# A rotary-embedding kernel on one Trainium2 core: half of tile 0 by SyncE's queue, GpSimd's loads after a wait, frequencies first

**Chip, cores, metric.** One core of one Trainium2 chip. The metric is the device time of the launch in microseconds, median of several runs. The profile covers a slightly shorter span of the same execution (83.5 us where the run took 85.3). The experiments ran on three chips (a, c and d on one, b on the second, e on the third), each beside its own runs of the kernel before (medians 85.43 to 85.64), so the ratios compare across them better than the times.

## The reference

```python
# x: (8, 8, 1024, 64) f32; freqs: (32,); positions: (1024,)
angles = np.outer(positions, freqs)
cos, sin = np.cos(angles), np.sin(angles)
x_first, x_second = x[..., :32], x[..., 32:]
out = concat([x_first * cos - x_second * sin, x_first * sin + x_second * cos], axis=-1)
```

It reads 16.8 MB and writes 16.8 MB.

## The kernel before

x is cut into 8 tiles of 2 MB (128 partitions of 64 rows x 64 values). GpSimd's DMA queue loads them and casts f32 to bf16, VectorE rotates in bf16, and GpSimd's queue stores them, casting back. SyncE's queue, which copies f32 without a cast, brings the first 16 of 64 rows of tile 0 and takes away the last 24 rows of tile 7. The parts that matter here:

```python
piece = 8
head = 2 * piece
x0 = singles.tile([P, head, d], f32)
for r in range(0, head, piece):                      # SyncE: 2 loads of 256 KB
    nc.sync.dma_start(out=x0[:, r:r + piece], in_=hbm(x, 0, r, r + piece))
# ... ScalarE's queue: positions (4 small loads), then freqs (1 small load)
for g in range(ntiles):                              # GpSimd: everything else of x
    lo = 0 if g else head
    nc.gpsimd.dma_start(out=xts[g][:, lo:], in_=hbm(x, g, lo))
# ... VectorE: positions * freqs, range reduction; ScalarE: sin_h, cos_h
nc.scalar.copy(out=xts[0][:, :head], in_=x0)         # f32 -> bf16
# ...
tail = 3 * piece
for g in [1, 0] + list(range(2, ntiles)):            # VectorE rotates, GpSimd stores
    hi = C if g < ntiles - 1 else C - tail
    ot = opool.tile([P, C, d], bf16, name="ot")[:, :hi]
    rotate(g, 0, hi, ot)
    ots.append(ot)
    nc.gpsimd.dma_start(out=hbm(out, g, 0, hi), in_=ot)
# ... the last `tail` rows as f32; SyncE waits for all stores but the last tile's, then:
#     sp.dma_start(...) for each piece of `last`
```

## Time and profile before

| | before |
|---|---|
| time, median of three runs (range); 85.64 with the fourth | 85.62 us (85.57 to 85.75) |
| span of the profile | 83.5 us |
| VectorE busy | 63.5 us |
| DMA: GpSimd's queue / SyncE's queue | 24.12 MB / 1.31 MB |
| VectorE ends / SyncE issues its last stores / last packet ends | 74.5 / 77.76 / 82.1 us |

In the profile's DMA rows a casting load is counted by the bf16 bytes that it writes, so 215 GB/s in the load half means 430 GB/s of reading. The timeline of GpSimd's queue (start, length, engine, line, operation, operands, count, and in brackets the idle time before and what ended it) shows when the loads are queued:

```profile
1.25 4.38 POOL L74 DMA_DIRECT2D xt<-in_x_dram  x8 [0.80 <-PEq L170]
```

All eight are queued one after another from 1.25 us on, so from then the queue stays deep. The waits of VectorE (line, what it waited for, total, times, longest) show the price of that: the tiny positions loads come late among the big packets.

```profile
DVE pos_i L76 <- DMA pos_i<-in_positions_dram: 8.0, 1, 8.0
```

### The profile page before, as it was taken

To read this page: it belongs to the slowest core of one execution; us is meant where nothing else is said; L and a number is where in the kernel's file an instruction comes from. 1 tells how busy PE (TensorE), PEld (TensorE's weight loads), DVE (VectorE), ACT (ScalarE), POOL (GpSimd) and SP (SyncE) were. 2 spreads that over 40 slices of the span, in tenths; PEclk is the share of its full clock that TensorE was granted. 3 is DMA by queue.
4 is the path that set the end of the run, shared out by engine and by line. 5 is a ranking of instruction groups with operands and counts; after the bars stand their busy time and mean duration, and the time that the engine had idled before them with its cause. 6 is when DMAs were issued, how large, how long until landed. Compare 5 with 4: busy or idle time off the path is not lost.

```text
span 83.5 us, 169 instructions
## 1 busy us (share of the span) xinstructions
DVE 63.5 (76%) x66; ACT 9.3 (11%) x6; POOL 8.8 (11%) x20
## 2 busy tenths in 40 slices
DVE  1000699649999999999999999999999999960000
ACT  0049200399300000000000000000000000000000
POOL 4960000000000202002001000200200202000000
DMA  1999999999999999999999999999999999999990
GB/s 35 217 217 214 204 224 216 204 231 200 231 200 224 216 208 228 200 231 200 200 412 408 455 408 439 432 428 447 400 455 416 439 432 432 439 408 425 424 371 28
DMA packets 3161, 25.47 MB, mean 305 GB/s; under 512 B 408, under 2 KB 472, under 8 KB 1240
## 3 DMA queue, kind: packets, MB, share of 16 engines
q0 software_dynamic: 2304, 24.12, 94.4%
q1 hardware_dynamic: 720, 1.31, 4.9%
q10 hardware_dynamic: 136, 0.03, 0.3%
q14 instruction: 1, 0.01, 0.0%
HBM read 16.81 MB, written 16.78 MB: 402 GB/s over the span
## 4 chain that ended last, share of the span: by engine, by line
DVE 75%; DMA 8%; ACT 2%; ACTq 2%; DVEq 1%; issue 1%
DVE t L114 11%; DVE t L115 11%; DVE ot L117 10%; DVE ot L119 10%; DVE ot L118 10%; DVE ot L116 10%; DMA pos_i<-in_positions_dram 8%; DVE turns L87 3%; DVE turns L93 3%; ACT sin_h L96 2%; ACTq L63 2%; DVE whole L91 1%; DVEq L170 1%; DVE last L117 1%; DVE last L118 1%; DVE last L116 1%
## 5 line engine op out<-in xcount | busy, mean ns | idle before, releaser
L114 DVE TENSOR_TENSOR t<-xt,sin_h 128x2048 bf16<-128x2048 bf16 (+2 forms) x9 | 9.9, 1097 | 2.0 <-ACT sin_h L96 2.0
L128 POOL DMA_DIRECT2D out_dram<-ot x8 | 4.3, 533 | 61.0 <-DVE ot L119 61.0
L115 DVE TENSOR_TENSOR t<-xt,sin_h 128x2048 bf16<-128x2048 bf16 (+2 forms) x9 | 9.9, 1097 | 0.0
L117 DVE TENSOR_TENSOR ot<-xt,cos_h 128x2048 bf16<-128x2048 bf16 (+1 forms) x8 | 9.3, 1165 | 0.0
L119 DVE TENSOR_TENSOR ot<-ot,t 128x2048 bf16<-128x2048 bf16 (+1 forms) x8 | 9.3, 1165 | 0.0
L118 DVE TENSOR_TENSOR ot<-ot,t 128x2048 bf16<-128x2048 bf16 (+1 forms) x8 | 9.3, 1164 | 0.0
L116 DVE TENSOR_TENSOR ot<-xt,cos_h 128x2048 bf16<-128x2048 bf16 (+1 forms) x8 | 9.3, 1164 | 0.0
L76 DVE LOAD_MASK_SELECT pos_i<-pos_i x1 | 0.0, 14 | 8.0 <-DMA pos_i<-in_positions_dram 8.0
L74 POOL DMA_DIRECT2D xt<-in_x_dram x8 | 4.4, 580 | 0.8 <-PEq L170 0.8
L96 ACT ACTIVATE sin_h<-turns 128x2048 bf16<-128x2048 f32 x1 | 1.9, 1909 | 7.1 <-DVE turns L93 7.1
L93 DVE TENSOR_TENSOR turns<-turns,whole 128x2048 f32<-128x2048 f32 x1 | 2.3, 2292 | 0.0
L87 DVE TENSOR_TENSOR turns<-pos_f,fturn 128x2048 f32<-128x2048 f32 x1 | 2.3, 2292 | 0.0
L99 ACT ACTIVATE cos_h<-whole,half_pi 128x2048 bf16<-128x2048 f32 x1 | 2.0, 2002 | 0.0
L98 ACT ACTIVATE whole<-turns 128x2048 f32<-128x2048 f32 x1 | 1.9, 1893 | 0.0
L101 ACT ACT_TABLE_LOAD x1 | 1.3, 1283 | 5.2 <-DMA x<-in_x_dram 5.2
L96 ACT ACT_TABLE_LOAD x1 | 1.3, 1283 | 0.0
L91 DVE TENSOR_SCALAR whole<-turns 128x2048 f32<-128x2048 f32 x1 | 1.2, 1226 | 0.0
L101 ACT CAST xt<-x 128x1024 bf16<-128x1024 f32 x1 | 1.0, 1044 | 0.0
L119 DVE TENSOR_TENSOR last<-last,t 128x768 f32<-128x768 f32 x1 | 0.9, 949 | 0.0
L117 DVE TENSOR_TENSOR last<-xt,cos_h 128x768 f32<-128x768 bf16 x1 | 0.9, 948 | 0.0
L116 DVE TENSOR_TENSOR last<-xt,cos_h 128x768 f32<-128x768 bf16 x1 | 0.9, 947 | 0.0
L118 DVE TENSOR_TENSOR last<-last,t 128x768 f32<-128x768 f32 x1 | 0.9, 947 | 0.0
(12 smaller groups left out, 1.6 us busy)
## 6 DMA issues: line engine op xcount, KB each, us to landing
out_dram<-ot POOLq DMA_DIRECT2D x7, 2048.0 KB, 17.5
xt<-in_x_dram POOLq DMA_DIRECT2D x7, 1024.0 KB, 25.1
out_dram<-ot POOLq DMA_DIRECT2D x1, 1280.0 KB, 10.3
xt<-in_x_dram POOLq DMA_DIRECT2D x1, 768.0 KB, 7.9
out_dram<-last SPq DMA_DIRECT2D x3, 256.0 KB, 3.8
x<-in_x_dram SPq DMA_DIRECT2D x2, 256.0 KB, 3.5
pos_i<-in_positions_dram ACTq DMA_DIRECT2D x4, 8.0 KB, 5.8
fr<-in_freqs_dram ACTq DMA_DIRECT2D x1, 0.5 KB
```

Of the source, the lines that this page charges most:

```text
L74: nc.gpsimd.dma_start(out=xts[g][:, lo:], in_=hbm(x, g, lo))
L87: nc.vector.tensor_mul(out=turns, in0=pos_f.to_broadcast([P, C, half]), in1=fturn.to_broadcast([P, C, half]))
L93: nc.vector.tensor_sub(out=turns, in0=turns, in1=whole)
L96: nc.scalar.activation(out=sin_h, in_=turns, func=Sin, scale=twopi)
L101: nc.scalar.copy(out=xts[0][:, :head], in_=x0)
L114: v.tensor_mul(out=t1, in0=xf, in1=sin)
L115: v.tensor_mul(out=t2, in0=xs, in1=sin)
L116: v.tensor_mul(out=of, in0=xf, in1=cos)
L117: v.tensor_mul(out=os_, in0=xs, in1=cos)
L118: v.tensor_sub(out=of, in0=of, in1=t2)
L119: v.tensor_add(out=os_, in0=os_, in1=t1)
L128: nc.gpsimd.dma_start(out=hbm(out, g, 0, hi), in_=ot)
```

## The change

The intent: let SyncE's queue fill the first microseconds with twice the data, keep GpSimd's deep queue away until the first quarter MB has landed, so that frequencies and positions come early and VectorE starts sooner, and shorten the f32 tail.

```diff
-    head = 2 * piece
+    head = 4 * piece
@@
+    fr = singles.tile([P, half], f32)                 # moved ahead of the positions
+    nc.vector.memset(fr, 0.0)
+    nc.scalar.dma_start(out=fr[0:P:32], in_=freqs[None, :].to_broadcast([P // 32, half]))
@@
+    pool = nc.gpsimd
+    tc.keep_in_program_order(pool.keepalive_nop(ins=[pool.lower_ap(x0[:, :piece])]))
     for g in range(ntiles):
         lo = 0 if g else head
-        nc.gpsimd.dma_start(out=xts[g][:, lo:], in_=hbm(x, g, lo))
+        tc.keep_in_program_order(pool.dma_start(out=xts[g][:, lo:], in_=hbm(x, g, lo)))
@@
-    nc.scalar.copy(out=xts[0][:, :head], in_=x0)
+    for r in range(0, head, 2 * piece):
+        nc.scalar.copy(out=xts[0][:, r:r + 2 * piece], in_=x0[:, r:r + 2 * piece])
@@
-    tail = 3 * piece
+    tail = 2 * piece
@@
-    for done in [pos_i, fr, x0] + ots[:-1]:
+    for done in [fr, pos_i, x0] + ots[:-1]:
```

More of the change, by code (lines that the diff above doesn't have):

```diff
@@ L66 @@
                         ap=[[C, chunks], [1, C], [1, 1]]))
-    fr = singles.tile([P, half], f32)
-    nc.vector.memset(fr, 0.0)
-    nc.scalar.dma_start(out=fr[0:P:32], in_=freqs[None, :].to_broadcast([P // 32, half]))
+    pool = nc.gpsimd
+    tc.keep_in_program_order(pool.keepalive_nop(ins=[pool.lower_ap(x0[:, :piece])]))
     for g in range(ntiles):
         lo = 0 if g else head
-        nc.gpsimd.dma_start(out=xts[g][:, lo:], in_=hbm(x, g, lo))
+        tc.keep_in_program_order(pool.dma_start(out=xts[g][:, lo:], in_=hbm(x, g, lo)))
     nc.vector.stream_shuffle(pos_i, pos_i, [i % chunks for i in range(32)])
```

## The prediction

> **What bounds the kernel now.** I read the page first, then the stretches of DMA share, then the chain of waits, the waits of SyncE's queue, and last the single DMA packets in the trace. Slices and queues come from the page:
>
> ```profile
> DVE  1000699649999999999999999999999999960000
> DMA  1999999999999999999999999999999999999990
> ...
> q0 software_dynamic: 2304, 24.12, 94.4%
> q1 hardware_dynamic: 720, 1.31, 4.9%
> ...
> HBM read 16.81 MB, written 16.78 MB: 402 GB/s over the span
> ```
>
> The reader is to see that the 16 DMA engines have work from the second slice to the last but one, while VectorE idles in the first ten slices and in the last four. q0 is GpSimd's queue (loads that cast f32 to bf16, stores that cast back), q1 is SyncE's (f32, 2 KB runs). The stretches say the same with sizes (columns: stretch and its length, busy us of VectorE, ScalarE and GpSimd with counts, clock, DMA share, GB/s; a casting load is counted by its bf16 bytes, so 214 there is about 428 GB/s of HBM reading):
>
> ```profile
> 0.00:1.80 1.80, 0.21 (x3) 0.00 (x0) 0.75 (x5) 1.00 0.01 2
> 1.80:4.20 2.40, 0.00 (x0) 0.00 (x0) 2.40 (x6) 1.00 0.91 221
> 4.20:42.20 38.00, 30.98 (x31) 9.32 (x6) 3.03 (x6) 1.00 1.03 214
> 42.20:81.40 39.20, 32.30 (x33) 0.00 (x0) 2.66 (x5) 1.00 1.06 427
> 81.40:82.20 0.80, 0.00 (x0) 0.00 (x0) 0.00 (x0) 1.00 0.23 85
> ```
>
> From 4.2 to 81.4 us DMA is full. The only soft stretch is 1.8 to 4.2: 221 GB/s of plain f32, half the rate, although the share reads 0.91 (some packets there take 300 to 1000 ns against a median of 84). The chain that ended last is misleading here. It gives VectorE 75%, starts with the positions and ends with VectorE's last instruction:
>
> ```profile
> 2.45 6.46 DMA pos_i<-in_positions_dram
> ...
> 73.63 0.87 DVEq L170
> ```
>
> That end, 74.5 us, is not what the output waits for. SyncE's three last stores were issued from 77.76, and its waits in the last 13 us are:
>
> ```profile
> SPq L137 <- DMA out_dram<-ot: 4.9, 1, 4.9
> SPq L137 <- DVE last L117: 4.9, 1, 4.9
> SPq L144 <- DMA out_dram<-last: 2.2, 2, 1.6
> ```
>
> Its last wait was for the store of the next-to-last tile, which landed at 77.7; VectorE was done 3.2 us before. So VectorE has 3.2 us of slack at the end, and the bound is the DMA stream: when it starts to be full, how many bytes it has left then, and how evenly the 16 engines finish.
>
> The packets make this exact. After the start every DMA engine does a 2 MB load in 4.87 us and a 2 MB store in 4.86 us, tile after tile. The mean completion over the engines is 8.27 us for the rest of tile 0, then 13.20, 18.07, 22.94 and so on, and the spread between first and last engine stays at 0.67 to 0.86 us from the first tile to the last. Whatever the start gives or takes is therefore still there at the end, undiluted.
>
> **What the Trainium skill says.** The page "DMA: Bandwidth & Descriptors", section "Issuing engines are not separate DMA queues", says that DMAs of all issuing engines run on the same 16 engines; the trace agrees, since q0, q1 and the small q10 together make a share of 1.0 and no more. Moving bytes from GpSimd's queue to SyncE's makes no bandwidth. The same page, "Latency and other measured facts", puts the first byte at about 0.6 us for SyncE's path and about 1 us for GpSimd's. In this trace SyncE's first packet starts 1.02 us after its issue (0.74 to 1.76), GpSimd's 2.67 us after (1.25 to 3.92). The second number is only an upper limit: on every engine the first q0 packet starts some 0.01 us after SyncE's second piece has ended there, so it may have stood ready. The same page, "Queues, rings and completion order", has each engine taking turns between queues by packets. The trace agrees in part: the second positions load, issued at 1.50, has its first packet only at 4.50, after q0's first ones. Since the engines went on from SyncE's first piece (ended at 2.56 to 3.50) to its second and not to q0, I read that q0 was not ready at about 2.6. That leaves 1.35 to 2.67 us from GpSimd's issue to its first packet; I take 2.0 as my estimate.
>
> **The change part by part.**
>
> *Start, SyncE.* Its loads grow from 2 to 4 pieces of 256 KB. The first two completed on the engines at a mean of 3.05 and 4.29 us, so 1.24 us a piece, where 8 packets of 84 ns each would be 0.67. The built program shows a wait that the diff doesn't: SyncE and ScalarE now issue nine loads where eight completion semaphores are to be had, so the fourth piece waits for the landing of the first. That landing was at 3.84 (0.74 plus the shortest landing time, 3.1); with frequencies first and GpSimd silent I expect about 3.7. The fourth piece's packets then run from some 4.7 to 5.4; the third fills the time before.
>
> *Start, GpSimd.* It waits for the same landing, so it issues at about 3.75 instead of 1.25, and q0's first packets come at 3.75 + 2.0 = 5.75, on all engines nearly at once, with a short hole before.
>
> *Break-even.* Half of tile 0 is then left to q0: 4.87 / 2 = 2.43 us, plus some 0.25 for the ramp and the positions' packets (before it was 3.98 for three quarters, that is 3.65, so 0.33 extra). Before, tile 0 was complete at 8.27 on the mean engine and 8.66 on the last. So q0 must start by 8.27 - 2.68 = 5.6 to be even on the mean engine, and by 8.66 - 2.68 = 6.0 on the last, which sets the end. With 5.75 on all of them: last engine 0.25 us earlier, mean 0.15 later. I count -0.1 us.
>
> *End.* `last` shrinks from 3 pieces to 2. A piece costs q1 0.67 us an engine (81.60 - 80.93 in the completion means), the same rows as part of a q0 store 4.86 / 8 = 0.61. Gain 0.06 us.
>
> *Frequencies first, positions unhindered.* The last of the positions completed at 8.42 and the frequencies at 9.26, amid q0's packets. Now q0 isn't there yet, and they should land by about 5.5 to 6, so VectorE starts at 5.5 to 6 instead of 9.04. The trigonometry is then ready some 3 us earlier (18 to about 15), near the landing of tile 1 (about 14). VectorE has slack already, so this only widens 3.2 us to about 6: 0 us. ScalarE now casts 2 x 1.04 us instead of 1 x 1.04, after the fourth piece lands at about 7, and is done well before it is wanted at 13. VectorE's smaller f32 tail (0.87 us instructions become about 0.58) is also hidden.
>
> Sum: 85.62 - 0.1 - 0.06, about 85.4.
>
> **Rivals.** *GpSimd's wait opens a hole.* If its latency really is 2.67 us, q0 starts at 3.84 + 2.67 = 6.5, 0.5 us after break-even on the last engine: 86.1. For: 2.67 is what the trace shows as issue to first packet, and the wait is new on the only path that carries 94% of the bytes. Against: the back-to-back packets show that q0 was queued behind q1. *The chain of waits is the truth:* positions 3 us earlier make the kernel 3 us shorter, 82.6. For: the page's 75% for VectorE. Against: DMA full for 77 us, and SyncE's last wait is for a store; I give it almost nothing. *SyncE's pieces run at full rate.* If the slow packets of 1.8 to 4.2 came from GpSimd writing its descriptors meanwhile, SyncE's megabyte arrives by 4.9 and GpSimd is quick too; with q0 at 5.2 the gain is 0.6 to 0.8: 84.9. *VectorE locks GpSimd out.* The skill's page "SBUF — State Buffer", section "SBUF: two separate sides", says that a VectorE instruction using both ports keeps GpSimd from writing descriptors. GpSimd would now write from 3.8 to 8.2 (8 x 0.54 us), when VectorE may be at its first small copies. Against: GpSimd's store issues took 0.53 us beside VectorE's bf16 stream as well, and each issue covers 4.9 us of transfer. At worst some 0.3 us.
>
> **Range and chances.** All the likely paths lie within 0.8 us of each other, because only the start moves. The whole soft stretch of before is worth about 1.2 us (2.4 us at half rate), less than 2% (1.7 us), so faster by 2% would need the spread of the engines to vanish too: 0.03. Slower by 2% needs q0 after 7.7: 0.03. Predicted 85.4, range 84.7 to 86.2.
>
> **What would show it.** Right: q0's first packets at 5.5 to 6.0 on all engines; the positions landed by 6 and VectorE starting then; still full DMA from there to the end; SyncE's last wait still for a tile's store, with VectorE done 5 to 6 us earlier. Wrong: an empty DMA stretch of more than 0.7 us before q0 starts (slower), or q0 at 5.2 and earlier (faster); tile loads longer than 4.87 us, from GpSimd starved of its port; or an end that moves with VectorE rather than with the stores.

## The result

**88.08 us (87.99 to 88.17) against 85.64 us: ratio 1.0284, interval 1.0266 to 1.0302, slower.** (Ratios here and below are the mean time of one kernel's fast runs over that of the other's of the same rounds, so not quite the ratio of the medians.) The prediction was 85.4, at most 86.2.

The page of the changed kernel, its slices and the bytes that they moved; the same row of the kernel before stands in the second fence:

```profile
DVE  1108991999999999999999999999999990000000
...
DMA  1899999999999999999999999999999999999950
GB/s 40 268 228 173 222 213 216 209 220 209 224 205 232 201 224 209 220 216 209 137 353 403 448 410 444 410 456 433 425 448 410 448 410 448 410 456 410 402 218 10
```

```profile
GB/s 35 217 217 214 204 224 216 204 231 200 231 200 224 216 208 228 200 231 200 200 412 408 455 408 439 432 428 447 400 455 416 439 432 432 439 408 425 424 371 28
```

VectorE starts earlier and is done earlier (seven idle slices at the end instead of four). The DMA engines still look busy throughout, but three places move fewer bytes: the fourth slice (173), the 20th (137) and the 39th (218). So the busy share does not show where the time went; the bytes do. Stretches of the kernel before, then of the changed one (length, busy us of VectorE, ScalarE and GpSimd, clock, DMA share, GB/s):

```profile
4.50:5.75 1.25, 0.00 (x0) 0.53 (x1) 1.12 (x3) 1.00 1.11 222
5.75:7.25 1.50, 0.00 (x0) 1.49 (x2) 0.00 (x0) 1.00 1.07 216
...
40.50:44.50 4.00, 4.00 (x5) 0.00 (x0) 0.00 (x0) 1.00 1.06 342
```

```profile
4.50:5.75 1.25, 0.00 (x0) 0.41 (x1) 1.25 (x3) 1.00 0.77 246
5.75:7.25 1.50, 0.46 (x3) 1.49 (x2) 1.50 (x4) 1.00 0.98 154
...
40.50:44.50 4.00, 4.00 (x4) 0.00 (x0) 0.53 (x1) 1.00 1.00 188
```

At 4.5 to 5.75 the kernel before moves 222 of bf16, which is some 440 of reading; the changed one 246 of plain f32. From 5.75 to 7.25 it is 154 against 216 although the share reads 0.98. At 40.5 to 44.5, where loads give way to stores, the changed kernel is slow once more.

The packet records give the account. Every DMA ends on each of the 16 engines with a 4-byte packet, so one can list when each engine was through with each transfer:

| completion on the engines, us | before: mean / last | changed: mean / last | difference: mean / last |
|---|---|---|---|
| rest of tile 0 | 8.27 / 8.66 | 9.14 / 9.81 | 0.87 / 1.15 |
| load of tile 6 | 37.54 / 38.00 | 38.46 / 39.21 | 0.92 / 1.21 |
| load of tile 7 | 42.52 / 43.09 | 44.29 / 45.40 | 1.77 / 2.31 |
| store of tile 6 | 76.56 / 77.10 | 78.33 / 80.06 | 1.77 / 2.96 |
| SyncE's last store | 81.60 / 82.13 | 83.55 / 85.04 | 1.95 / 2.91 |

Between the rows the two kernels go at the same pace (4.87 us a load, 4.86 a store). So the profiled span lost 0.9 us at the start, another 0.85 in tile 7's load, and the last engine fell 0.65 us further behind during the stores. (The profiled run of the kernel before, 85.30 us, is 0.3 below its median, so the spans differ by 2.8 us where the medians differ by 2.4.) That last step is one event: at 52.68 us an 8 KB instruction fetch of 0.34 us went through the queue of one DMA engine, its next packet took 969 ns instead of 642, and this engine was the last one already. Before, the same fetch came at 56.36 on an engine that was not the last.

Where GpSimd's queue starts, and what VectorE and SyncE wait for, in the changed kernel (timeline, then the waits of VectorE, then those of SyncE's queue: its fourth load at the start, and the last 14 us):

```profile
4.32 4.38 POOL L77 DMA_DIRECT2D xt<-in_x_dram  x8 [3.88 <-DMA x<-in_x_dram]
```

```profile
DVE pos_i L79 <- DMA pos_i<-in_positions_dram: 2.5, 1, 2.5
DVE t L118 <- DMA xt<-in_x_dram: 2.1, 1, 2.1
```

```profile
SPq L55 <- DMA x<-in_x_dram: 1.4, 1, 1.4
...
SPq L141 <- DMA out_dram<-ot: 9.6, 2, 4.8
SPq L148 <- DMA out_dram<-last: 2.8, 1, 2.8
```

The intent is reached: VectorE has its positions at 6.75 instead of 9.04 and rotates from 15.29 instead of 17.90. But then it waits for tile 1, and at the end SyncE waits for stores alone; VectorE is done at 71.35, and SyncE's last stores are issued at 80.62. VectorE's gain went into slack, and GpSimd's first load went from 1.25 to 4.32 us.

### The profile page after: what moved, and what is told of

The parts are those of the page before. It is cut to its first block, busy times and chain, and to the rows that moved or that the text cites. A ratio compares the mean times of both kernels' runs of the same rounds, so it can differ in the third digit from the quotient of the medians.

```text
span 86.3 us, 175 instructions
## 1 busy us (share of the span) xinstructions
DVE 63.0 (73%) x66; ACT 10.3 (12%) x7; POOL 8.8 (10%) x20
## 4 chain that ended last, share of the span: by engine, by line
DVE 64%; DMA 15%; issue 1%; POOL 1%; DVEq 1%; POOLq 0%
DMA xt<-in_x_dram 12%; DVE t L118 11%; DVE t L119 11%; DVE ot L123 10%; DVE ot L121 10%; DVE ot L122 10%; DVE ot L120 10%; DMA x<-in_x_dram 3%; POOL xt L77 1%; DVEq L174 1%; DVE last L121 1%; DVE last L122 1%; DVE last L120 1%; DVEq L118 0%; POOLq L74 0%
## 5 line engine op out<-in xcount | busy, mean ns | idle before, releaser
L105 ACT CAST xt<-x 128x1024 bf16<-128x1024 f32 x2 | 2.0, 1042 | 0.0
L121 DVE TENSOR_TENSOR last<-xt,cos_h 128x512 f32<-128x512 bf16 x1 | 0.7, 682 | 0.0
L123 DVE TENSOR_TENSOR last<-last,t 128x512 f32<-128x512 f32 x1 | 0.7, 682 | 0.0
L120 DVE TENSOR_TENSOR last<-xt,cos_h 128x512 f32<-128x512 bf16 x1 | 0.7, 681 | 0.0
```

Of the source, the lines that this page charges most:

```text
L105: nc.scalar.copy(out=xts[0][:, r:r + 2 * piece], in_=x0[:, r:r + 2 * piece])
L120: v.tensor_mul(out=of, in0=xf, in1=cos)
L121: v.tensor_mul(out=os_, in0=xs, in1=cos)
L123: v.tensor_add(out=os_, in0=os_, in1=t1)
```

## The experiments

"Slow packets" below are tile load packets of more than 700 ns (the usual one takes 625) that start at 40 us or later. "Tile 0" is the mean completion of its rest on the engines. Both come from the one profiled run of each kernel; the times are medians of four runs (three for the kernel before, one for e3).

| kernel | us | ratio to before (interval) | tile 0 | slow packets |
|---|---|---|---|---|
| before | 85.62 | 1 | 8.27 | 9 |
| changed | 88.08 | 1.0284 (1.0266 to 1.0302) | 9.14 | 36 |
| a1 wait only | 87.43 | 1.0225 (1.0191 to 1.0259) | 10.63 | 6 |
| a2 changed, no wait | 86.77 | 1.0128 (1.0079 to 1.0177) | 7.66 | 0 |
| a3 tile 7 loaded third | 88.52 | 1.0333 (1.0274 to 1.0391) | 9.26 | 44 |
| a4 frequencies and tail only | 86.18 | 1.0074 (1.0039 to 1.0108) | 8.63 | 7 |
| b1 before, wait ahead of tile 1 | 85.39 | 0.9975 (0.9943 to 1.0007) | 8.28 | 12 |
| b2 changed, wait ahead of tile 1 | 86.01 | 1.0077 (1.0017 to 1.0137) | 7.89 | 0 |
| b3 changed, pieces 3 and 4 merged | 86.60 | 1.0131 (1.0094 to 1.0167) | 9.63 | 30 |
| b4 changed, again | 88.36 | 1.0339 (1.0297 to 1.0380) | 9.36 | 38 |
| c1 changed, stores after loads | 90.27 | 1.0541 (1.0479 to 1.0603) | 9.56 | 0 |
| c2 changed, third store after loads | 87.96 | 1.0291 (1.0231 to 1.0351) | 9.36 | 35 |
| c3 b1, third store after loads | 85.44 | 1.0005 (0.9967 to 1.0043) | 8.28 | 9 |
| d1 changed, VectorE later | 88.41 | 1.0355 (1.0284 to 1.0426) | 9.14 | 34 |
| d2 changed, second store after loads | 88.57 | 1.0343 (1.0281 to 1.0406) | 9.38 | 37 |
| d3 wait only, again | 87.50 | 1.0225 (1.0172 to 1.0278) | 10.53 | 9 |
| e1 wait and four pieces | 87.23 | 1.0193 (1.0148 to 1.0239) | 9.13 | 36 |
| e2 wait, frequencies, tail | 87.48 | 1.0239 (1.0205 to 1.0274) | 10.68 | 11 |
| e3 stores after loads, again | 89.65 (one run) | | 9.37 | 0 |

All give the right result. d1 and e1 each had one run of four that is called slow (89.02 and 88.96), which the ratios leave out and the medians do not; the fast runs alone have medians of 88.27 and 86.97. In a program on one core "slow" says only that the run was over 1.5% above the kernel's fastest, so it may also be the kernel's own scatter.

### First: which part costs the time

**a1, the wait alone.** Edit, on the kernel before:

```diff
+    tc.keep_in_program_order(pool.keepalive_nop(ins=[pool.lower_ap(x0[:, :piece])]))
     for g in range(ntiles):
```

> The kernel before plus GpSimd's wait for SyncE's first piece, nothing else (two pieces on SyncE, tail of 3). Theory: the wait is the cost. GpSimd's first load issues at about 4.3 us instead of 1.25 and its first packets come 1.5 us later, at 5.8, with only 0.5 MB there to fill the time, so tile 0 completes at a mean of about 9.8 instead of 8.27, and the total is 87.1 or more (1.5 from the start alone), up to 88.5 if the slow stretch at 41 to 44 us comes with it. Rival (the four pieces on SyncE cost the time): about 85.6.

Measured 87.43. GpSimd's first load issues at 4.32 and its first packet starts at 5.70; tile 0 completes at 10.63. The stretches after SyncE's two pieces are in:

```profile
4.50:5.75 1.25, 0.52 (x5) 1.16 (x1) 1.25 (x3) 1.00 0.29 30
5.75:7.25 1.50, 1.43 (x3) 1.47 (x3) 1.50 (x4) 1.00 0.79 102
7.25:10.50 3.25, 3.18 (x3) 0.98 (x1) 1.45 (x3) 1.00 1.04 196
```

There is the hole (share 0.29), and after it a slow ramp: 102, then 196, where the kernel before runs at 216. The start alone costs 2.36 us in the profiled runs, more than expected, and the median goes up by 1.9 (87.43 against 85.53 in the fast runs of the same rounds). The wait alone is enough to make the kernel slower; a2 must show whether the four pieces are another.

**a2, the changed kernel without the wait.**

```diff
-    tc.keep_in_program_order(pool.keepalive_nop(ins=[pool.lower_ap(x0[:, :piece])]))
```

> The changed kernel without GpSimd's wait; four pieces, frequencies first and tail of 2 stay. Theory (the wait is the cost): GpSimd's packets ready by about 2.8 us, tile 0 complete by about 8.3 on the mean engine, total 85.3 to 85.7. Rival (the four pieces, or the fourth that waits for the first, are the cost): 86.5 to 88.

Measured 86.77, in the rival's range, though not because the loads start late: tile 0's part by GpSimd is early (7.66). The four pieces of SyncE have to share the engines with GpSimd's deep queue: the fourth is through 5.6 us after the third on the mean engine (11.96 to 17.54). Eight packets of 84 ns, each taking turns with one of GpSimd's (4.87 / 8 = 0.61 us), would make 8 x 0.69 = 5.5; this is an estimate, and it fits. The waits of ScalarE, VectorE and, at the end, SyncE:

```profile
ACT xt L104 <- DMA x<-in_x_dram: 8.9, 1, 8.9
...
DVE pos_i L78 <- DMA pos_i<-in_positions_dram: 7.5, 1, 7.5
DVE t L117 <- ACT sin_h L98: 6.1, 1, 6.1
...
SPq L144 <- DVE last L122: 1.4, 1, 1.4
```

ScalarE waits for the fourth piece, which is through on the last engine only at 19.58 us, and the sine stands behind that cast in ScalarE's order; VectorE rotates from 24.25 and ends at 80.32, so now VectorE sets the end. The wait that costs the time is thus what lets the four pieces land early (the fourth by 6.36 in the changed kernel).

**a4, the two small parts alone.** The edit on the kernel before, in words:

```diff
-    # freqs fetched after the positions;  tail = 3 * piece
+    # freqs fetched before the positions; tail = 2 * piece
```

> The kernel before with the two small parts alone: frequencies fetched first, and a tail of 2 pieces. Theory: neither touches the DMA stream, 85.4 to 85.7. Rival (VectorE's earlier or later start shifts the stores and makes the slow stretch at 41 to 44 us): above 86.3 with slow loads of tile 7.

Measured 86.18, 0.6 us more than before, not by slow loads of tile 7 (7 packets). With the frequencies first, SyncE's second piece is through on the last engine at 9.75 instead of 4.82 us, behind GpSimd's packets, and the engines come out of tile 0 unevenly (last 9.77 instead of 8.66). a2 and b2, which also fetch the frequencies first and let GpSimd start at 1.25, show it too (8.34 and 7.87); the kernel before, b1 and c3 do not (4.75 to 4.82). So a small load on another queue can change which queue gets an engine first. The changed kernel, where GpSimd starts later, does not show it (4.26).

### Second: can the start be had without the hole

**b1 and b2: the wait moved one load later,** on the kernel before and on the changed one.

```diff
-    tc.keep_in_program_order(pool.keepalive_nop(...))   # (b2; b1 had none)
     for g in range(ntiles):
         lo = 0 if g else head
+        if g == 1:
+            tc.keep_in_program_order(pool.keepalive_nop(ins=[pool.lower_ap(x0[:, :piece])]))
```

> The kernel before (two pieces, tail of 3, positions first) with GpSimd's wait placed after the load of tile 0's rest, ahead of tile 1's. Theory (the loss at the start is a hole in GpSimd's queue, its wait, 0.63 us to the issue and 1.5 us to the first packet): tile 0's rest is queued at 1.25 us as before and keeps the engines busy until about 8.2, tile 1 is queued at about 4.3 and ready at 5.8, so no hole: tile 0 complete at 8.0 to 8.4, total 85.2 to 85.8. Rival (the wait harms in itself, for instance by the position of GpSimd's descriptor writing): over 86.3.

Measured 85.39, as the theory had it. The timeline of GpSimd's queue:

```profile
1.24 0.67 POOL L77 DMA_DIRECT2D xt<-in_x_dram  x1 [0.80 <-PEq L173]
4.60 3.70 POOL L77 DMA_DIRECT2D xt<-in_x_dram  x7 [2.69 <-DMA x<-in_x_dram]
```

Tile 1 is queued at 4.60, while tile 0 keeps the engines busy until 8.3, and tile 0 completes at 8.28 as before. The same wait shows no cost one load later: it is the hole that costs, not the waiting. The interval of its ratio reaches over 1, so this is no version shown to be faster.

> The changed kernel (four pieces, frequencies first, tail of 2) with the wait moved between tile 0's rest and tile 1. Theory: no hole, and the pieces of SyncE have only 8 packets of tile 0 an engine beside them, not a deep queue as in the run without the wait, so the fourth piece lands by 8 instead of 19.6 us; 2 MB are complete by about 7.6 to 8.2 (GpSimd's share and SyncE's pieces), tile 1 by 12.6 to 13.2, total 85.0 to 85.7. Rival (the four pieces lose the turn to GpSimd's packets even so): fourth piece after 10 us, total over 86.3.

Measured 86.01 with a fourth piece that is through at 19.78 us on the last engine and VectorE starting its rotations at 24.45: the theory fell, and the rival was right about the piece, not about its total of over 86.3. The waits, as in a2:

```profile
ACT xt L106 <- DMA x<-in_x_dram: 8.6, 1, 8.6
...
DVE t L119 <- ACT sin_h L100: 6.0, 1, 6.0
```

**b3, no ninth semaphore.** The third and fourth piece become one load.

```diff
-    for r in range(0, head, piece):
-        nc.sync.dma_start(out=x0[:, r:r + piece], in_=hbm(x, 0, r, r + piece))
+    for r, n in [(0, piece), (piece, piece), (2 * piece, 2 * piece)]:
+        nc.sync.dma_start(out=x0[:, r:r + n], in_=hbm(x, 0, r, r + n))
```

> The changed kernel with SyncE's third and fourth piece as one load of 512 KB, so that eight semaphores are enough and no piece waits for the first. Theory (the wait for a semaphore costs little, since GpSimd's packets are ready only at 5.83): SyncE's bytes are in by 5.3 instead of 5.9, GpSimd's first packets start at 5.8 on all engines instead of 5.8 to 6.4, tile 0 complete at a mean of 8.9 instead of 9.14 and the engines closer together; total 87.2 to 87.9. Rival (the ninth load's wait is the main cost): under 86.5. If the slow loads at 41 to 44 us hang on the spread of the engines, they are gone here and the total is near 86.5 too; the profile tells which.

Measured 86.60, 1.8 us less than the changed kernel on the same chip in the same rounds (b4, 88.36), between the two theories. The start is not why: GpSimd issued at 4.76 here and tile 0 completed later (9.63). The engines are closer together, though: the last one leaves tile 7's load 0.44 us after the mean instead of 1.11, and everything 0.59 instead of 1.49. The slow packets stayed (30), so they do not hang on the spread. So 0.9 of the 1.1 us by which its profiled span is shorter (85.2 against 86.3) is evenness of the engines. (This compares one profiled run of each; b3's, 86.96, was its slowest, and what its other runs gained beyond that is not explained.) That the ninth load's wait makes the changed kernel uneven is only argued: b4, which has it too, came out at 1.31, but a3, c2, d1 and e1, which also have it, at 0.85 to 0.94. More than half of the loss goes with this edit, and its cause stays open.

### Third: why tile 7's load is slow

**b4, the changed kernel again.** No edit.

> The changed kernel once more, unedited. If its slow loads at 41 to 44 us belong to the kernel: there again, with 30 or more packets over 700 ns, total 87.9 to 88.3. If they come and go: fewer, with a total near 87.2, which is 0.85 less.

Measured 88.36 and 38 slow packets; they belong to the kernel.

**a3, tile 7 loaded third.**

```diff
-    for g in range(ntiles):
+    for g in [0, 1, ntiles - 1] + list(range(2, ntiles - 1)):
```

> The changed kernel, but tile 7 is loaded third instead of last. It tells what the slow loads at 41 to 44 us (tile 7's) hang on. If on the addresses of tile 7: slow packets at 16 to 20 us now, none at 41 to 44, same total of about 88. If on the time or on being the last load before the stores: tile 6's packets are slow at 41 to 44. In both cases the start is unchanged (tile 0 complete at about 9.1).

Measured 88.52 and 44 slow packets, all of tile 6, the last one now. It is not tile 7's addresses.

**c1, e3, c2, c3, d2: fewer stores in the queue.** GpSimd waits for the last tile's landing ahead of its first (c1 and e3), second (d2) or third store (c2; c3 on b1).

```diff
+        if len(ots) == N:                       # N = 0, 1 or 2
+            tc.keep_in_program_order(pool.keepalive_nop(ins=[pool.lower_ap(xts[ntiles - 1])]))
         ots.append(ot)
-        nc.gpsimd.dma_start(out=hbm(out, g, 0, hi), in_=ot)
+        tc.keep_in_program_order(pool.dma_start(out=hbm(out, g, 0, hi), in_=ot))
```

> The changed kernel, but GpSimd queues no store before tile 7's load has landed (about 44 us). Theory (stores standing in the queue behind the last load slow it): no slow packets at 41 to 44, tile 7 complete at a mean of 43.4 instead of 44.3; then a hole of about 2 us until the first store's packets, so the total stays at 88 to 89. Rival (the slow stretch comes from something else at that place or time): 30 or more slow packets as before, and the total 89.5 to 90.5.

> The changed kernel with no store queued before the loads have landed, once more. If stores in the queue are needed for the slow stretch: no slow packet at 41 to 44 us again. If its absence was luck: 30 or more.

No slow packet, twice, as the theory had it; c1's total of 90.27 lay above the theory's 88 to 89. e3's stretches (its run is of unknown state, being single):

```profile
41.00:43.00 2.00, 2.00 (x3) 0.00 (x0) 0.00 (x0) 1.00 1.05 221
43.50:47.00 3.50, 3.50 (x4) 0.00 (x0) 1.17 (x3) 1.00 0.11 42
```

The load runs at its full 221 up to its end; then comes the hole until the first store's packets (the first store completes 8.8 us after the load in c1, where a store takes 4.86), which makes both slower than the changed kernel.

> The changed kernel, but the third store (and all after it) waits until tile 7's load has landed; two stores stand in the queue at the end of the loads, enough for 9.7 us. Theory (three or more stores queued behind the last load slow it; the two kernels that had two showed no slow packet): slow stretch gone, total 86.4 to 87.3. Rival: slow packets as before and 88 to 88.4.

> The changed kernel with one store only in the queue until tile 7's load has landed. If stores behind the last load slow it and their number counts: fewer slow packets than with two (35). If any store is enough: 30 or more. If stores have nothing to do with it and the run without was luck: 30 or more too, so only a low count tells. No hole is expected (one store lasts 4.9 us), total 86.8 to 88.5.

35 and 37 slow packets, 87.96 and 88.57: one store in the queue is enough. The theory of their number fell.

> The kernel before with the wait between tile 0 and tile 1 (85.39 us) and the same holding of the third store. It had 12 slow packets at 40.5 to 41.6, worth 0.15 us. Theory: none, total 85.1 to 85.3. Rival: no change, 85.4.

85.44, 9 slow packets: no change there either.

**d1, VectorE later,** by two idle products ahead of the sine.

```diff
+    spare = singles.tile([P, C, half], f32)
+    for _ in range(2):
+        tc.keep_in_program_order(nc.vector.tensor_mul(out=spare, in0=turns, in1=whole))
     nc.vector.tensor_sub(out=turns, in0=turns, in1=whole)
```

> The changed kernel with two idle products of 2.3 us on VectorE ahead of the sine, so that its rotations begin at about 19.9 instead of 15.3 us; the loads are untouched. If the slow stretch hangs on when VectorE's work and stores come: under 15 slow packets, total 86.6 to 87.4 (VectorE ends at 76, still hidden). Rival (it hangs on the loads' own start): 30 or more slow packets, total 87.9 to 88.6.

Rotations from 19.31 us, yet 34 slow packets and 88.41: moving VectorE's work by 4 us changed nothing.

**d3, the wait alone again, and e1, e2: the wait with four pieces, and with the small parts.** d3 has no edit against a1; e1 is a1 with `head = 4 * piece` and the two casts of ScalarE; e2 is a4 with the wait.

> The kernel before with GpSimd's wait alone, once more. If the small number of slow packets (6) belongs to this kernel: under 15 again and 87.2 to 87.6. If it comes and goes: up to 40, and 88 or more.

> The kernel before with the wait and four pieces on SyncE; positions before frequencies and the tail of 3 stay. If the pieces bring the slow last load: 30 or more slow packets at 41 to 44 us, total 87.8 to 88.6, like the whole change. Rival (the small parts bring it): under 15, total about 86.8.

> The kernel before with the wait and the two small parts; two pieces on SyncE stay. If the pieces bring the slow last load: under 15 slow packets, total 87.2 to 87.6, like the wait alone. Rival (the small parts bring it): 30 or more, and 88.2 or more.

9, 36 and 11 slow packets. The stretch from 41.0 to 43.5 us of the changed kernel, then of e1, then of e2:

```profile
41.00:43.50 2.50, 2.50 (x3) 0.00 (x0) 0.53 (x1) 1.00 1.05 154
```

```profile
41.00:43.50 2.50, 2.50 (x3) 0.00 (x0) 0.53 (x1) 1.00 1.04 157
```

```profile
41.00:43.50 2.50, 2.50 (x3) 0.00 (x0) 0.00 (x0) 1.00 0.97 193
```

Behind the wait, the slow last load comes with the four pieces, not with the small parts. e1's total was missed: 87.23 where I had expected 87.8 to 88.6, although its start, its slow packets and its mean engine (83.53 at the end) are those of the changed kernel; its last engine was done at 84.47 instead of 85.04, and its unprofiled fast runs were shorter still (86.89 and 86.97).

## Why the prediction was wrong

**What held.** The bound was right: DMA fills both kernels, SyncE's last long wait is for a store in both, and VectorE's earlier start went into slack. VectorE rotates from 15.29 us, for which I had said about 15, close to tile 1's landing; VectorE has the positions at 6.75 (said: 5.5 to 6); the first piece landed at about 3.69, when GpSimd's wait let go (said: 3.7); tiles 1 to 6 keep 4.87 us a load. The rival in which the chain's 75% of VectorE is the truth fell. So did the one in which SyncE's pieces run at full rate once GpSimd is silent: with it silent they still moved only 164 GB/s at 2.5 to 3.0 us and 238 in the half microsecond after, and 351 around 4.0. Tile loads of unchanged length show no sign of VectorE locking GpSimd out.

**The step that failed first** is the sum of the start: "With 5.75 on all of them: last engine 0.25 us earlier, mean 0.15 later. I count -0.1 us." Measured: mean 0.87 later, last engine 1.15 later. Term by term on the mean engine:

- Issue. I took GpSimd to issue 0.05 us after the landing; it issued 0.63 us after (3.69 to 4.32). The kernel before had shown the same gap: its start barrier let go at 0.63 and its first load issued at 1.25.
- Latency. I took 2.0 us to the first packet; it is 1.51 (4.32 to 5.83). The two errors nearly cancel, which is luck: 5.83 instead of 5.75 for the first engine.
- All engines at once. They started at 5.83 to 6.44, mean 6.14, which is 0.39 more than 5.75. In a1, where SyncE's pieces were through by 4.14, GpSimd's first packets are spread as well (5.70 to 6.59, mean 5.97, after an issue at the same 4.32), so most of this is the start of GpSimd's queue itself. The fourth piece, which waits for a semaphore and was through at 5.59 to 6.36, may account for the 0.17 between the two means; e1, which has it too, needs 1.62 us from issue to the mean first packet, a1 1.65, the changed kernel 1.82.
- Ramp. Half of tile 0 took 3.00 us (6.14 to 9.14) where I had 2.68; ten of the first packets took 741 to 1076 ns against a median of 329. That is 0.32 more. a1 shows it larger: 4.66 us for three quarters, 3.98 before.

0.15 + 0.39 + 0.32 = 0.86 of the 0.87 measured. The rival "GpSimd's wait opens a hole" had the right cause, though its latency of 2.67 us and its 86.1 were not what came. The runs show the cause: the wait alone costs 1.90 us (a1) and 1.88 (d3), and one load later none can be seen (b1). The chance of 0.03 for slower by 2% rested on q0 after 7.7; q0 came by 6.44 and the kernel was slower by 2.8% all the same, since the loss did not end with the start.

**The second step that failed** is "Whatever the start gives or takes is therefore still there at the end, undiluted". It takes the loss to stay the same. In the changed kernel it doubled on the mean engine, in tile 7's load (0.92 to 1.77 us), and on the last engine went to 2.91. Six profiled runs of the changed kernel's kind with a store in the queue had this slow load (changed, a3, b4, c2, d1, d2), as had e1 and, less, b3, always with half of tile 0 on SyncE's queue and GpSimd silent before it. The last load took 5.75 to 5.88 us on the mean engine in the first seven, 5.46 in b3, and 4.87 to 5.05 everywhere else. None with two pieces had more than 12 slow packets, and the two runs without a store in the queue had none. The prediction had no such term. It also took the engines' spread as fixed and even hoped to shrink it; it grew, since slow packets hit the engines unequally and an instruction fetch fell on the last one.

**The end.** `last` with two pieces was to gain 0.06 us; the mean engine lost 0.18 there instead: the second piece was through 0.98 us after the first where 0.67 was counted. In e2, a2 and c1, whose engines finish together or nearly so, it is 0.65 to 0.66. Why is not shown.

**What stays open.** Why four pieces behind the wait make the last load slow, when a store stands in the queue. Its addresses, the 4 us of VectorE's time that d1 moved, the number of stores from one up and a wide spread of the engines (b3 is slow with 0.90 us between first and last engine at tile 6, a4 is not with 1.70) are excluded; a2 and b2 also have four pieces and stores queued (from 33.7 us) but no slow packet, with another start of GpSimd's queue and much later stores. When the loads run is not separated from the pieces: tile 0 completes at 9.13 to 9.63 in every kernel with the slow load, and in those with stores queued and no slow load by 8.63 or from 10.53 on. No run shifts the loads and leaves the pieces alone. That a2 and b2 finish tile 6 at 38.18 and 38.25 on the mean engine, close to e1's 38.37, speaks against it, no more. Nor is the share of the small parts settled: next to the wait alone they cost nothing (e2 87.48, a1 87.43), while the changed kernel, which is e1 with them, is about 0.8 us slower than e1's fast runs by the ratios (1.0284 and 1.0193, not from the same rounds); the two profiles differ in the last engine, not in the mean, and e1's run of 88.96, left out as slow, lies above the changed kernel. Last, no run has the four pieces behind the wait without either the slow load or another hole, so what the slow load costs in the total (0.85 us) comes from packet records alone.

## What to carry to other kernels

Where DMA is the bound, a wait put into the deep queue costs the landing, the issue and the first-packet latency as a hole, and a slow ramp behind it, unless the queue has work in front of it that lasts longer; put such a wait behind the first transfer (b1), unless what it was to protect needs the engines to itself meanwhile (b2). Judge by bytes moved and by when each engine is through, not by busy shares, and check the built program for waits that no line of the source shows. An earlier start of an engine with slack was worth nothing here (VectorE was done 9.3 us before SyncE's last stores), although it fills 64% of the chain of waits.

## What the Trainium skill lacked or had wrong

- "DMA: Bandwidth & Descriptors", Latency and other measured facts: first byte about 0.6 us by SyncE's path and about 1 us by GpSimd's. Measured from issue to the first engine's first packet: 1.02 us for SyncE, and 1.38 for GpSimd in a1, where SyncE's pieces were through before (1.65 on the mean engine). A load of GpSimd that follows a wait pays 0.63 us before its issue on top (3.69 to 4.32), which the page doesn't have.
- The same page has no slow start of a queue. In the changed kernel SyncE's loads moved 287 GB/s at 2.0 to 2.4 us, fell to 134 at 2.6 to 2.8 and came to 358 only from 3.6 on; ten of GpSimd's first packets took 741 to 1076 ns against a median of 329.
- The same page, Queues, rings and completion order, has engines take turns by packets. It gives no figure for what this does to a small transfer next to a deep queue: a 256 KB piece beside GpSimd's queue took 5.6 us after the piece before it, and the fourth was through at 19.58 us (a2), with that queue started later at 6.36 (the changed kernel).
- No page read for this case has the slow last load: with a store queued behind it, a tile's load ran at 154 instead of some 215 GB/s (bf16 bytes) from 41.0 to 43.5 us; with none, at 221 until its end.
- The same page names a row of queues for instruction refill, and no page read for this case says what a fetch costs the transfers of its DMA engine: one 8 KB fetch cost its DMA engine 0.67 us (342 ns and 327 ns on the next packet).
